# Seven block products for a down projection, with a later start of each group and bias tables made first

## The chip, the cores and the metric

One core of one Trainium2 chip runs the kernel. The metric is the device time of one execution in microseconds, here the median of three runs. TensorE is called PE (its weight loads PEld), VectorE DVE, ScalarE ACT, GpSimd POOL and SyncE SP, as in the profile.

## The reference, cut to what matters

The network has two layers; each is a feed-forward block, a mixer (attention, dilated attention, gated delta rule) and a second feed-forward block. The change concerns the four feed-forward blocks and the small bias tables of the dilated attention.

```python
def swiglu(x, wg, wu, wd):
    return (jax.nn.silu(x @ wg) * (x @ wu)) @ wd

for l in range(DEPTH):   # DEPTH = 2, x: 512 x 1024, wg and wu: 1024 x 2816, wd: 2816 x 1024, float32
    h = h + 0.5 * swiglu(rms_norm(h, ffn1_norm[l]), ffn1_w_gate[l], ffn1_w_up[l], ffn1_w_down[l])
    h = h + hybrid_mixer(rms_norm(h, mix_norm[l]), rel_bias, ...)
    h = h + 0.5 * swiglu(rms_norm(h, ffn2_norm[l]), ffn2_w_gate[l], ffn2_w_up[l], ffn2_w_down[l])
```

## The kernel before

Everything is held transposed: eight tiles x[0..7] of 128 features by 512 tokens, so a matmul has a 128x128 block of weights as its loaded operand and 512 tokens as its moving one. Each float32 product is made of three matmuls (mm3, L214 to L218): weights and activations are split into a high part of type float32r and the rest, and high times high, high times rest and rest times high are summed in PSUM. The split of a weight block (weight, L200) is a DMA on SP, a copy on ACT (L210) and a subtraction on DVE (L211); it is issued at high priority, so it stands early in those queues.

A feed-forward block (ffn, L270) goes over 22 row blocks f of the hidden layer in groups of 8, 7 and 7. For each f it makes the gate and the up product (8 mm3 each, tile pg), then s and h on DVE, ACT and POOL (L294 to L298), and the split of h (hh, hl, L301 and L302). After each group come eight down products, one for each output tile dm: the group's 7 or 8 mm3 into tile pd, and an addition of half of it to x[dm] on DVE (L310). That is 8 x 22 x 3 = 528 down matmuls of 512 columns in a block, 2,112 in the program. In the last group norm_add (L231) follows each dm: it scales, splits and squares x[dm] for the next norm, and norm_end (L247) sums the squares on PE.

The bias tables: build_lines (L176) loads three small tables, makes one row by head with a matmul (pline, L193), writes it to memory and spreads it over 128 rows there (L198). It is called inside the first feed-forward block, before its fourth f (L278).

The program is written through a scheduler that orders each engine's instructions; an engine then works through its own queue in that order and waits at the head of it.

Of the kernel before, what the change touches and what calls it, by code (L numbers as in the profile page):

```python
# [19 lines left out]
P = 128  # L20
# [6 lines left out]
FGROUPS = [8, 7, 7]  # L27
AHEAD = 1
HOLD = 5
SCAN_AT = (0, 2, 4, 6, 8, 10, 12, 14)  # L30
# [82 lines left out]
class Body:  # L113
    def __init__(self, tc, ctx, a):
# [11 lines left out]
        self.ones = self.const.tile([P, P], F32, name="ones")  # L126
# [37 lines left out]
    def load_consts(self):  # L164
# [4 lines left out]
        self.pick = self.const.tile([64, 6 * P], F32R, name="pick")  # L169
        self.ident16 = self.const.tile([P, P], BF16, name="ident16")  # L170
# [5 lines left out]
    def build_lines(self, ps=None):  # L176
        nc = self.nc
        self.line = self.dram.tile([6, P * (2 * T + 1)], F32, name="line")
        one = self.dram.tile([6, NLINE], F32, name="oneline")
        with self.tc.tile_pool(name="lines", bufs=1) as lp, (nullcontext(ps) if ps else self.banks("lp")) as ps:  # L180
            pick = lp.tile([64, 6 * P], F32, name="pick")
            nc.scalar.dma_start(out=pick, in_=self.a["pick"])
            nc.scalar.activation(out=self.pick, in_=pick, func=AF.Copy)
# [6 lines left out]
            for c0 in range(0, NLINE, T):  # L190
                n = min(T, NLINE - c0)
                p = ps.tile([P, T], F32, name="pline", tag="aux", bufs=3)
                nc.tensor.matmul(out=p[0:6, :n], lhsT=rb, rhs=tab[:, c0:c0 + n], start=True, stop=True)  # L193
                nc.vector.tensor_scalar(out=row[:, c0:c0 + n], in0=p[0:6, :n], scalar1=-1.0, scalar2=None, op0=ALU.mult)
            nc.scalar.dma_start(out=one, in_=row)
        for h in range(6):
            dst = self.line[h:h + 1, :].rearrange("o (p n) -> (o p) n", n=2 * T + 1)[:, 0:NLINE]
            nc.scalar.dma_start(out=dst, in_=one[h:h + 1, :].to_broadcast([P, NLINE]))  # L198

    def weight(self, src, n, tiles=None):  # L200
        nc = self.nc
        if tiles is None:
            raw = self.wp.tile([P, n], F32, name="wraw", tag="wraw", bufs=2)
            hi = self.wp.tile([P, n], F32R, name="whi", tag="whi")
            lo = self.wp.tile([P, n], F32R, name="wlo", tag="wlo")
        else:
            raw, hi, lo = tiles
# [6 lines left out]
    def mm3(self, out, w, x, first, last):  # L214
        nc = self.nc
        nc.tensor.matmul(out=out, lhsT=w[0], rhs=x[0], start=first, stop=False)  # L216
        nc.tensor.matmul(out=out, lhsT=w[0], rhs=x[1], start=False, stop=False)  # L217
        nc.tensor.matmul(out=out, lhsT=w[1], rhs=x[0], start=False, stop=last)  # L218
# [12 lines left out]
    def norm_add(self, n, i):  # L231
# [6 lines left out]
        n["x"].append((hi, lo))  # L238
        if i == 0:
# [7 lines left out]
    def norm_end(self, n, ps):  # L247
        nc = self.nc
        pb = ps.tile([P, T], F32, name="pssq", tag="aux", bufs=3)
        for t in range(NT):  # L250
            for r in (0, 64):
                nc.tensor.matmul(out=pb[r:r + 64, t:t + 1], lhsT=n["acc"][:, t * P + r:t * P + r + 64],
                                 rhs=self.ones[:, 0:1], start=True, stop=True)
# [5 lines left out]
        pr = ps.tile([P, T], F32, name="prow", tag="aux", bufs=3)  # L259
# [10 lines left out]
    def ffn(self, n, wgu, wd, nxt):  # L270
        nc, tc = self.nc, self.tc
        scope = lambda name, bufs: tc.tile_pool(name=name, bufs=bufs, reuse_waits="tile")
        with scope("fs", 2) as fs, scope("fh", max(FGROUPS)) as fh, self.banks("fp") as ps:
            f0 = 0
            for gi, ng in enumerate(FGROUPS):
                hs = []
                for f in range(f0, f0 + ng):
                    if self.hold and f == 3:  # L278
                        self.build_lines(ps)
                    pp = []  # L280
                    for which in range(2):
                        hold = self.tc.issue_after(self.hold) if self.hold and f + which == 1 else nullcontext()
                        with hold:
                            hi, lo = self.weight(wgu[f, :, which], D)
                        p = ps.tile([P, T], F32, name="pg", tag="mm")
                        pp.append(p)
                        for k in range(KD):
                            c = slice(k * P, k * P + P)
                            self.mm3(p, (hi[:, c], lo[:, c]), n["x"][k], k == 0, k == KD - 1)
# [769 lines left out]
```

## Time and profile before

| | us |
|---|---|
| runs, median (three, 2237.58 to 2239.57) | 2239.5 |
| the profiled execution, its own time | 2234.65 |
| its span in the profile | 2232.6 |
| PE busy | 2179.1 |
| PE weight loads busy | 1745.9 |
| DVE, ACT, POOL busy | 1138.8, 789.5, 483.7 |

The span is what the trace covers of an execution. An engine is busy while it works on an instruction; matmuls overlap each other, so their length (397 ns for 512 columns) is more than their spacing, and it is the spacing that counts for time.

### The profile page before, as it was taken

How to read it: one execution, taken by the hardware profiler on the slowest of the kernel's cores; microseconds unless marked ns; L12 is line 12 of the kernel's file. 1: busy time of each engine (PE TensorE's matmuls, PEld its weight loads, DVE VectorE, ACT ScalarE, POOL GpSimd, SP SyncE). 2: the span in 40 equal slices, each digit the busy share in tenths (PEclk: the TensorE clock that was granted, in tenths of full speed). 3: DMA queues.
4: the chain of work that ended last, by engine and by line, in shares of the span. 5: the costliest groups of instructions: out<-in, count | busy, mean ns of one | idle time of the engine just before them, and what ended most of it. 6: DMA issues, size and time to landing. Idle time of an engine off the chain costs nothing.

```text
span 2232.6 us, 30294 instructions
## 1 busy us (share of the span) xinstructions
PE 2179.1 (98%) x12212; PEld 1745.9 (78%) x12212; DVE 1138.8 (51%) x1881; ACT 789.5 (35%) x1153; POOL 483.7 (22%) x490
## 2 busy tenths in 40 slices
PE   7999999998999999999999999999989999999999
PEld 5888887778777888888788888877787778888887
DVE  5333334688677533333443333347795765333333
ACT  4222223524565322222332222235345643222221
POOL 3101012217253210101121010123073531101010
PEclk9999999999999999999999999999999999999999
DMA  5433333232302333333233333332331033333333
GB/s 172 127 95 94 96 95 120 81 82 85 92 18 95 95 94 95 95 90 98 86 95 94 95 91 98 92 126 67 100 103 47 28 105 92 94 93 93 96 92 102
DMA packets 93076, 206.82 MB, mean 93 GB/s; under 512 B 38561, under 2 KB 39073, under 8 KB 92936
## 3 DMA queue, kind: packets, MB, share of 16 engines
q1 hardware_dynamic: 91168, 199.98, 30.0%
q10 hardware_dynamic: 1768, 4.91, 0.8%
q8 instruction: 96, 1.57, 0.3%
q14 instruction: 44, 0.36, 0.1%
HBM read 193.83 MB, written 14.18 MB: 93 GB/s over the span
## 4 chain that ended last, share of the span: by engine, by line
PE 88%; DVE 8%; ACT 2%; issue 1%; DMA 1%; POOL 0%; ACTq 0%; SPq 0%; DVEq 0%; POOLq 0%
PE pg L218 15%; PE pg L216 15%; PE pg L217 15%; PE pd L218 7%; PE pd L216 7%; PE pd L217 7%; PE pc L216 2%; PE pc L218 2%; PE pc L217 2%; PE pav L900 1%; PE ppt L894 1%; DVE wlo L211 1%; PE pwo L217 1%; PE pwo L216 1%; PE pwo L218 1%
## 5 line engine op out<-in xcount | busy, mean ns | idle before, releaser
L210 ACT ACTIVATE whi<-wraw 128x1024 fp32r<-128x1024 f32 (+3 forms) x344 | 351.4, 1022 | 1228.9 <-PE pg L217 651.7
L216 PE MATMUL pg<-xh,whi 128*128 128x512 f32 x1408 | 558.0, 397 | 8.5 <-ACT xh L236 8.3
L217 PE MATMUL pg<-xl,whi 128*128 128x512 f32 x1408 | 558.4, 397 | 2.3 <-DVE xl L237 2.2
L218 PE MATMUL pg<-xh,wlo 128*128 128x512 f32 x1408 | 557.8, 396 | 0.8 <-DVE wlo L211 0.8
L211 DVE TENSOR_TENSOR wlo<-wraw,whi 128x1024 fp32r<-128x1024 f32 (+3 forms) x344 | 408.4, 1187 | 89.0 <-ACT whi L210 83.5
L296 POOL TENSOR_TENSOR s<-s,rstd 128x512 f32<-128x512 f32 x88 | 152.7, 1737 | 1146.5 <-ACT s L295 1146.5
L216 PEld LDWEIGHTS pg<-xh,whi 128*128 128x128 f32 x1408 | 265.2, 188 | 73.2 <-ACT xh L236 8.3
L217 PEld LDWEIGHTS pg<-xl,whi 128*128 128x128 f32 x1408 | 265.0, 188 | 68.5 <-DVE xl L237 5.3
L218 PEld LDWEIGHTS pg<-xh,wlo 128*128 128x128 f32 x1408 | 265.1, 188 | 65.1 <-DVE wlo L211 1.9
L218 PE MATMUL pd<-hh,wlo 128*128 128x512 f32 x704 | 278.7, 396 | 0.9 <-DVE wlo L211 0.9
L216 PE MATMUL pd<-hh,whi 128*128 128x512 f32 x704 | 278.5, 396 | 0.0
L217 PE MATMUL pd<-hl,whi 128*128 128x512 f32 x704 | 278.4, 395 | 0.0
L310 DVE SCALAR_TENSOR_TENSOR x<-pd,x 128x512 f32<-128x512 f32 x96 | 66.3, 691 | 284.6 <-PE pd L218 284.6
L298 DVE TENSOR_TENSOR h<-pg,s 128x512 f32<-128x512 f32 x88 | 60.9, 691 | 287.8 <-PE pg L218 281.3
L294 DVE TENSOR_TENSOR s<-pg,rstd 128x512 f32<-128x512 f32 x88 | 60.6, 691 | 229.9 <-PE pg L218 229.7
L218 PEld LDWEIGHTS pd<-hh,wlo 128*128 128x128 f32 x704 | 132.3, 188 | 34.0 <-DVE wlo L211 2.2
L217 PEld LDWEIGHTS pd<-hl,whi 128*128 128x128 f32 x704 | 132.4, 188 | 31.9
L216 PEld LDWEIGHTS pd<-hh,whi 128*128 128x128 f32 x704 | 132.4, 188 | 31.7
L753 PE MATMUL pgr<-wlo,xh 128*128 128x384 f32 (+1 forms) x256 | 92.0, 360 | 11.2 <-DVE wlo L211 11.1
L884 POOL TENSOR_TENSOR prob<-prob,sm 128x512 f32<-128x512 f32 x80 | 84.6, 1066 | 78.5 <-DVE sm L883 63.5
L245 POOL TENSOR_TENSOR acc<-acc,sq 128x512 f32<-128x512 f32 x42 | 67.5, 1606 | 132.6 <-ACT sq L244 132.0
L754 PE MATMUL pgr<-whi,xl 128*128 128x384 f32 (+1 forms) x256 | 90.7, 354 | 0.0
(235 smaller groups left out, 2702.0 us busy)
## 6 DMA issues: line engine op xcount, KB each, us to landing
wraw<-in_gu_dram SPq DMA_DIRECT2D x176, 512.0 KB, 3.6
wraw<-in_wd_dram SPq DMA_DIRECT2D x64, 448.0 KB, 3.3
wraw<-in_wd_dram SPq DMA_DIRECT2D x32, 512.0 KB, 3.6
wraw<-in_w_c_dram SPq DMA_DIRECT2D x24, 512.0 KB, 3.6
wraw<-in_w_gb_dram SPq DMA_DIRECT2D x24, 384.0 KB, 3.1
wraw<-in_w_o_dram SPq DMA_DIRECT2D x14, 512.0 KB, 3.7
bias<-line SPq DMA_DIRECT2D x12, 448.0 KB, 5.0
saved<-x SPq DMA_DIRECT2D x16, 256.0 KB, 2.0
```

The lines of the kernel that those rows point to most:

```text
L210: nc.scalar.activation(out=hi, in_=raw, func=AF.Copy)
L211: nc.vector.tensor_tensor(out=lo, in0=raw, in1=hi, op=ALU.subtract)
L216: nc.tensor.matmul(out=out, lhsT=w[0], rhs=x[0], start=first, stop=False)
L217: nc.tensor.matmul(out=out, lhsT=w[0], rhs=x[1], start=False, stop=False)
L218: nc.tensor.matmul(out=out, lhsT=w[1], rhs=x[0], start=False, stop=last)
L245: nc.gpsimd.tensor_tensor(out=n["acc"], in0=n["acc"], in1=sq, op=ALU.add)
L296: nc.gpsimd.tensor_tensor(out=s, in0=s, in1=n["rstd"], op=ALU.mult)
L298: nc.vector.tensor_tensor(out=h, in0=pp[1], in1=s, op=ALU.mult)
L310: nc.vector.scalar_tensor_tensor(out=self.x[dm], in0=p, scalar=0.5, in1=self.x[dm], op0=ALU.mult, op1=ALU.add)
L753: nc.tensor.matmul(out=o, lhsT=xh[:, tk], rhs=lo[:, wc], start=False, stop=False)
L754: nc.tensor.matmul(out=o, lhsT=xl[:, tk], rhs=hi[:, wc], start=False, stop=kk == KD - 1)
L884: nc.gpsimd.tensor_tensor(out=pb, in0=pb, in1=sm.to_broadcast([P, T]), op=ALU.mult)
```

## The change

The down projection works on pairs of row blocks and pairs of output tiles. Hidden row blocks f = j and f = j + 11 (HALF) form pair j; output tiles dm and dm + 4 form a pair; the 512 tokens are cut into two halves of 256. Each such 2x2 by 2x2 block product takes seven products instead of eight, on sums and differences of the blocks:

- up makes, for pair j, both gate and up products (unchanged matmuls), then three subtractions on DVE for the combined tokens, and seven split blocks of 256 columns (hh and hl, in a call with four and one with three of them).
- down loads the four weight blocks of a group for the pair dm in two DMAs (ra, rb), makes s1, s2, s4 on POOL and one difference on DVE, splits 7 blocks of weights (ra, sa, rb, s4), and runs seven products of 256 columns on three PSUM tiles, pu, py and pz. pu is added to x by DVE after each of its four products, while PE keeps summing into it. There are 4 steps dm a group, and a group has 3, 4 and 4 pairs.
- a group's down steps come after the up product of one pair more than the group holds (hs[0:ng] is used, one pair stays over). In the last group there is no such pair, and the first step (late) leaves the last pair's matmuls of its first three products to the end of them.
- build_lines is called before the first feed-forward block, right after the constants; the tables' six spread writes stay inside the block, as spread_lines. The next norm takes its tiles in the order 0, 4, 1, 5, 2, 6, 3, 7. In the program there are 4 x 4 x 11 x 7 x 3 = 3,696 down matmuls of 256 columns.

```diff
-FGROUPS = [8, 7, 7]
+FPAIRS = [3, 4, 4]
+HALF = FF // P // 2
+TH = T // 2
+RAWS, SPLITS, MM = 2, 2, 6
...
+            hs, j0 = [], 0
+            for gi, ng in enumerate(FPAIRS):
+                last = gi == len(FPAIRS) - 1
+                for j in range(j0 + len(hs), min(j0 + ng + 1, HALF)):
+                    hs.append(self.up(n, wgu, j, fs, fh, ps))
+                for dm in range(KD // 2):
+                    self.down(wd[dm, :, j0 * 4 * P:(j0 + ng) * 4 * P], dm, hs[0:ng], fs, ps, last and dm == 0)
+                    if last and nxt is not None:
                         self.norm_add(nxt, dm)
-                f0 += ng
+                        self.norm_add(nxt, dm + KD // 2)
+                j0, hs = j0 + ng, hs[ng:]
...
+        t = fs.tile([P, 3, TH], F32, name="ht", bufs=1)
+        sub = lambda out, x, y: nc.vector.tensor_tensor(out=out, in0=x, in1=y, op=ALU.subtract)
+        sub(t[:, 0:2], h[:, 1::2], h[:, 0:2])
+        sub(h[:, 1], h[:, 3], t[:, 0])
+        sub(t[:, 2], h[:, 2], h[:, 1])
+        hh = fh.tile([P, 7, TH], F32R, name="hh")
+        hl = fh.tile([P, 7, TH], F32R, name="hl")
+        for o, src in ((slice(0, 4), h), (slice(4, 7), t)):
+            nc.scalar.activation(out=hh[:, o], in_=src, func=AF.Copy)
+            nc.vector.tensor_tensor(out=hl[:, o], in0=src, in1=hh[:, o], op=ALU.subtract)
+        return hh, hl
+
+    def down(self, src, dm, hs, fs, ps, late):
...
+            ra, rb = self.raw(2 * m), fs.tile([P, 2 * m], F32, name="wrb")
+            nc.sync.dma_start(out=ra, in_=src[:, 0:2 * m])
+            nc.sync.dma_start(out=rb, in_=src[:, 2 * m:4 * m])
+            a11, a12, a22, a21 = ra[:, 0:m], ra[:, m:], rb[:, 0:m], rb[:, m:]
+            sa = fs.tile([P, 2 * m], F32, name="wsa")
+            s4 = fs.tile([P, m], F32, name="wsb", bufs=1)
+            s1, s2 = sa[:, 0:m], sa[:, m:]
+            nc.gpsimd.tensor_tensor(out=s1, in0=a21, in1=a22, op=ALU.add)
+            nc.gpsimd.tensor_tensor(out=s2, in0=s1, in1=a11, op=ALU.subtract)
+            nc.gpsimd.tensor_tensor(out=s4, in0=a12, in1=s2, op=ALU.subtract)
+            nc.vector.tensor_tensor(out=a21, in0=a11, in1=a21, op=ALU.subtract)
+            wa, wb = self.halves(ra), self.halves(sa)
+            wc, wd = (self.halves(v, tuple(fs.tile([P, v.shape[-1]], F32R, name=nm + x, bufs=1) for x in "hl"))
+                      for v, nm in ((rb, "wc"), (s4, "wd")))
...
+        begin = (u, wa, 0, 0), (z, wb, 0, 4), (y, wa, 1, 2)
+        if late:
+            for js in (range(ng - 1), range(ng - 1, ng)):
+                for args in begin:
+                    product(*args, True, js)
+        else:
+            product(*begin[0], True)
+            product(*begin[1], True)
+        h5 = fs.tile([P, TH], F32, name="p5", bufs=1)
+        add(0, u)
+        nc.scalar.activation(out=h5, in_=z, func=AF.Copy, scale=0.5)
+        product(u, wb, 1, 1, False)
+        add(1, u)
+        if not late:
+            product(*begin[2], True)
+        add(0, y)
+        product(u, wc, 1, 5, False)
+        add(3, u)
+        nc.gpsimd.tensor_tensor(out=x[3], in0=x[3], in1=h5, op=ALU.add)
+        product(z, wd, 0, 3, False)
+        add(1, z)
+        product(u, wc, 0, 6, False)
+        add(2, u)
...
             k.load_consts()
+            k.build_lines()
```

The scheduler decides where these stand in the queues; three places matter below. The first is ACT's queue in the program's first microseconds (xh and sq belong to the first norm, whi is the high part of a gate or up weight block). Before:

```order
L161 DMA small_71<-in_small_dram 128x96
L182 DMA pick<-in_pick_dram 64x768
L186 DMA rb<-in_rel_bias_dram 32x6
L210 ACT_TABLE_LOAD
L210 ACTIVATE whi<-wraw 128x1024
L188 DMA tab<-in_line_table_dram 33x1023
L236 ACTIVATE xh<-x,small_71 128x512
```

and with the change, from the last xh on:

```order
L256 ACTIVATE xh<-x,small_71 128x512
L164 DMA small_147<-in_small_dram 128x96
L170 DMA consts<-in_consts_dram 128x1794
L265 ACTIVATE sq<-x 128x512
L175 DMA pick<-in_pick_dram 64x768
L265 ACTIVATE sq<-x 128x512
L176 ACTIVATE pick<-pick 64x768
L190 DMA rb<-in_rel_bias_dram 32x6
L192 DMA tab<-in_line_table_dram 33x1023
L199 DMA oneline<-row 6x1023
L205 DMA line<-oneline 128x1023 x6
L216 ACTIVATE whi<-wraw 128x1024 x2
```

The loads of rb and tab have moved from the front of the queue to behind the copy of pick. PE's queue now begins with the matmuls that need them:

```order
L197 MATMUL pline<-tab,rb 6x512
L197 MATMUL pline<-tab,rb 6x511
L236 MATMUL pg<-xh,whi 128x512
L237 MATMUL pg<-xl,whi 128x512
L238 MATMUL pg<-xh,wlo 128x512
```

Before, pline stood behind 98 other rows of this queue; now the first pg matmul stands behind pline.

The second place is DVE's queue where the last group of a feed-forward block begins (s and h belong to the last pair; wlo is the rest part of wa, then of wb):

```order
L329 TENSOR_TENSOR s<-pg,rstd 128x512
L231 TENSOR_TENSOR wlo<-wraw,whi 128x1024
L333 TENSOR_TENSOR h<-pg,s 128x512
L335 TENSOR_TENSOR ht<-h 128x512
L231 TENSOR_TENSOR wlo<-wsa,whi 128x1024
L335 TENSOR_TENSOR h<-h,ht 128x256
L335 TENSOR_TENSOR ht<-h 128x256
L361 TENSOR_TENSOR wrb<-wraw,wrb 128x512
L343 TENSOR_TENSOR hl<-h,hh 128x1024
L343 TENSOR_TENSOR hl<-ht,hh 128x768
L376 SCALAR_TENSOR_TENSOR x<-pu,x 128x256
```

and before, at the same place:

```order
L294 TENSOR_TENSOR s<-pg,rstd 128x512
L211 TENSOR_TENSOR wlo<-wraw,whi 128x896
L298 TENSOR_TENSOR h<-pg,s 128x512
L211 TENSOR_TENSOR wlo<-wraw,whi 128x896
L302 TENSOR_TENSOR hl<-h,hh 128x512
L310 SCALAR_TENSOR_TENSOR x<-pd,x 128x512
```

Between h and the first addition to x there were two instructions; now there are seven, one of which (wrb) waits for POOL.

The third place is PE's queue inside a down step, at the change from one product to the next (with buffer numbers, since pu is used four times):

```order
L238 MATMUL pu_1823<-hh_1646,wlo_1808 128x256
L236 MATMUL pz_1825<-hh_807,whi_1811 128x256
L237 MATMUL pz_1825<-hl_808,whi_1811 128x256
L236 MATMUL py_1824<-hh_807,whi_1807 128x256
L237 MATMUL py_1824<-hl_808,whi_1807 128x256
L238 MATMUL py_1824<-hh_807,wlo_1808 128x256
```

where before stood

```order
L216 MATMUL pd_839<-hh_265,whi_834 128x512
L217 MATMUL pd_839<-hl_266,whi_834 128x512
L216 MATMUL pd_807<-hh_797,whi_802 128x512
L218 MATMUL pd_839<-hh_265,wlo_835 128x512
L216 MATMUL pd_839<-hh_337,whi_834 128x512
```

Each matmul has half as many columns and, as before, a weight load of its own; products of different steps are interleaved.

## Rows read from the trace of the kernel before

**Rows 1.** page, head, busy time and chain of waits by engine

```profile
span 2232.6 us, 30294 instructions
PE 2179.1 (98%) x12212; PEld 1745.9 (78%) x12212; DVE 1138.8 (51%) x1881; ACT 789.5 (35%) x1153; POOL 483.7 (22%) x490
...
PE 88%; DVE 8%; ACT 2%; issue 1%; DMA 1%; POOL 0%; ACTq 0%; SPq 0%; DVEq 0%; POOLq 0%
```

**Rows 2.** windows: us, PE, PEld, DVE, ACT, POOL busy (count), clock, DMA share, GB/s

```profile
232.00:271.00 39.00, 39.00 (x169) 31.43 (x168) 15.00 (x17) 8.39 (x9) 0.00 (x0) 1.00 0.32 93
```

**Rows 3.** PE timeline (start us, us), first and last of 168 down matmuls of a group

```profile
232.16 0.40 PE L216 MATMUL pd<-hh,whi 128*128 128x512 f32 x1
...
271.13 0.39 PE L218 MATMUL pd<-hh,wlo 128*128 128x512 f32 x1
```

**Rows 4.** PE timeline: 384 columns, first and last of seven; then the 128-column ones

```profile
514.98 0.33 PE L753 MATMUL pgr<-wlo,xh 128*128 128x384 f32 x1
...
516.02 0.34 PE L753 MATMUL pgr<-wlo,xh 128*128 128x384 f32 x1
...
36.54 1.06 PE L261 MATMUL prow<-consts,rcol 128*128 128x128 f32 x8
...
L261 PE MATMUL prow<-consts,rcol x8: 273/275/275, 36.5 to 37.3; 128*128 128x128 f32 x8
```

**Rows 5.** weight loads by form: busy us, mean ns

```profile
L216 PEld LDWEIGHTS pd<-hh,whi 128*128 128x128 f32 x704 | 132.4, 188 | 31.7
L261 PEld LDWEIGHTS prow<-consts,rcol 128*128 128x128 f32 x48 | 6.3, 190 | 0.5
```

**Rows 6.** DVE by form: busy us, mean ns | idle before

```profile
L211 DVE TENSOR_TENSOR wlo<-wraw,whi 128x1024 fp32r<-128x1024 f32 x254 | 311.9, 1228 | 69.7 <-ACT whi L210 69.0
L211 DVE TENSOR_TENSOR wlo<-wraw,whi 128x768 fp32r<-128x768 f32 x24 | 23.3, 972 | 13.6 <-ACT whi L210 13.6
L302 DVE TENSOR_TENSOR hl<-h,hh 128x512 fp32r<-128x512 f32 x88 | 60.2, 686 | 0.8 <-ACT hh L301 0.7
L537 DVE TENSOR_TENSOR kd<-pt,ek 128x384 f32<-128x384 f32 x16 | 7.9, 547 | 1.0 <-PE pt L534 1.0
L776 DVE TENSOR_TENSOR qkv<-qkv,rqg 128x256 f32<-128x256 f32 x24 | 8.6, 416 | 0.1
```

**Rows 7.** ACT by form: busy us, mean ns | idle before

```profile
L210 ACT ACTIVATE whi<-wraw 128x1024 fp32r<-128x1024 f32 x254 | 269.3, 1061 | 966.8 <-PE pg L217 587.8 <-PE pd L217 174.0 <-issue 75.5
L210 ACT ACTIVATE whi<-wraw 128x768 fp32r<-128x768 f32 x24 | 20.2, 843 | 27.2 <-PE pgr L754 17.1 <-DMA wraw<-in_w_gb_dram 6.5 <-DVE wlo L211 3.3
```

**Rows 8.** POOL: one line, ns min/median/max; then the 384-column form, mean ns

```profile
L296 POOL TENSOR_TENSOR s<-s,rstd x88: 1277/1790/2452, 39.8 to 2185.7; 128x512 f32<-128x512 f32 x88
...
L562 POOL TENSOR_TENSOR gt<-g,consts 128x384 f32<-128x384 f32 x16 | 17.0, 1067 | 7.5 <-DVE g L469 4.7 <-PE pe L566 2.8
```

**Rows 9.** windows of the gate and up matmuls alone, from the start

```profile
0.00:30.00 30.00, 17.98 (x58) 11.62 (x59) 0.00 (x0) 1.00 0.62 189
```

**Rows 10.** timeline of the start, all engines

```profile
8.29 0.79 PE L216 MATMUL pg<-xh,whi 128*128 128x512 f32 x1 [8.29 <-ACT xh L236]
17.67 0.44 ACTq L167 DMA_DIRECT2D consts<-in_consts_dram  x1
...
23.34 0.21 DVE L171 CAST ident<-consts 128x128 bf16<-128x128 f32 x1
...
39.86 1.88 PE L193 MATMUL pline<-tab,rb 33*6 33x512 f32 x4
...
43.96 0.30 ACTq L195 DMA_DIRECT2D oneline<-row  x1
...
46.57 1.19 ACTq L198 DMA_DIRECT2D line<-oneline  x2
```

**Rows 11.** DMA issues: count, KB each, median us to landing

```profile
consts<-in_consts_dram ACTq DMA_DIRECT2D x1, 897.0 KB, 4.7
pick<-in_pick_dram ACTq DMA_DIRECT2D x1, 192.0 KB, 7.4
```

More of the change, by code (lines that the diff above doesn't have):

```diff
@@ L169, in load_consts @@
         self.pick = self.const.tile([64, 6 * P], F32R, name="pick")
+        with self.tc.tile_pool(name="picks", bufs=1, reuse_waits="tile") as lp:
+            pick = lp.tile([64, 6 * P], F32, name="pick")
+            nc.scalar.dma_start(out=pick, in_=self.a["pick"])
+            nc.scalar.activation(out=self.pick, in_=pick, func=AF.Copy)
         self.ident16 = self.const.tile([P, P], BF16, name="ident16")
@@ L174, in load_consts, with build_lines @@
         nc.vector.tensor_copy(out=self.mask16[:, 1], in_=self.c["mask_r"])
-    def build_lines(self, ps=None):
+    def build_lines(self):
         nc = self.nc
         self.line = self.dram.tile([6, P * (2 * T + 1)], F32, name="line")
[L179 to L183, printed above, removed]
+        self.one = one = self.dram.tile([6, NLINE], F32, name="oneline")
+        with self.tc.tile_pool(name="lines", bufs=1, reuse_waits="tile") as lp, self.banks("lp") as ps:
             rb = lp.tile([33, 6], F32, name="rb")
@@ L202, in weight @@
         if tiles is None:
-            raw = self.wp.tile([P, n], F32, name="wraw", tag="wraw", bufs=2)
-            hi = self.wp.tile([P, n], F32R, name="whi", tag="whi")
-            lo = self.wp.tile([P, n], F32R, name="wlo", tag="wlo")
+            raw = self.raw(n)
+            hi, lo = self.split(n)
         else:
@@ new lines, in up @@
+    def up(self, n, wgu, j, fs, fh, ps):
+        nc = self.nc
+        h = fs.tile([P, 4, TH], F32, name="h")
+        for half in range(2):
+            f = j + half * HALF
+            if self.hold and (j, half) == (2, 0):
+                self.spread_lines()
+            pp = []
+            for which in range(2):
+                first = j == half == 0
+                hold = self.tc.issue_after(self.hold) if self.hold and first and which else nullcontext()
+                with hold:
+                    hi, lo = self.weight(wgu[f, :, which], D)
+                p = ps.tile([P, T], F32, name="pg", tag="mm", bufs=MM)
+                pp.append(p)
+                for i, k in enumerate(n["order"]):
+                    c = slice(k * P, k * P + P)
+                    self.mm3(p, (hi[:, c], lo[:, c]), n["x"][k], i == 0, i == KD - 1)
+                if which == 0:
+                    if first:
+                        self.norm_end(n, ps, 2)
+                    s = fs.tile([P, T], F32, name="s")
+                    nc.vector.tensor_tensor(out=s, in0=p, in1=n["rstd"], op=ALU.mult)
+                    nc.scalar.activation(out=s, in_=s, func=AF.Silu)
+                    nc.gpsimd.tensor_tensor(out=s, in0=s, in1=n["rstd"], op=ALU.mult)
+            hv = h[:, 2 * half:2 * half + 2].rearrange("p a t -> p (a t)")
+            nc.vector.tensor_tensor(out=hv, in0=pp[1], in1=s, op=ALU.mult)
+        t = fs.tile([P, 3, TH], F32, name="ht", bufs=1)
[9 more added lines that the diff above has]
+        return hh, hl
```

106 lines of the change are left out of this document (50 added, 56 removed).

## The prediction, made before the changed kernel had run

> **What bounds the kernel now.** The page comes first: PE is busy 98% of the span and the chain of waits runs through PE for 88% of it, so what the kernel loses or gains is PE time [rows 1]. The windows of single stages say the same of the stage that changes: in 39 us of the second down group of the first block PE is busy for all 39, DVE for 15.0, ACT for 8.4 and POOL not at all [rows 2]. DVE and POOL have room there, PE has none. What one matmul costs is read not from its length (0.40 us) but from starts in the timeline: 168 down matmuls begin between 232.16 and 271.13, which is 38.97 / 167 = 0.2333 us each [rows 3]. So all 2,112 down matmuls cost 492.7 us, and nothing else in their stage is on the path.
>
> **What the products cost.** The change puts 3,696 matmuls of 256 columns in place of 2,112 of 512. No 256-column float32r matmul is in the trace, so its price lies between neighbours. Six steps of 384 columns take 516.02 - 514.98 = 1.04 us, 0.1733 each [rows 4]. From 512 to 384 columns the spacing falls by 0.0600; a second fall of the same size gives 0.1133 for 256. Whether the weight load, one for every matmul, lets it fall so far is seen at the eight 128-column matmuls of prow: first start to last end 1.06 us, less the last one's 0.274, over seven, is 0.112 each, although each of them brings a 128x128 load of 190 ns mean, as long as the 188 of the down projection's [rows 4, 5]. So loads can follow each other every 0.112 us. I take 0.1133: 418.8 us, a gain of **73.9**. The ends are 0.112 (gain 78.7) and half of the 512-column price, 0.1167 (gain 61.4).
>
> A rule of the Trainium skill speaks against this. Its page "TensorE: Matmul & The Clock Gate", section "The mechanism" of Part 3, says that weight loads overlap running matmuls only when they go to another row group, which these full-height loads never do. By it a load of about 107 ns (its section "LDWEIGHTS (loading the stationary operand)": columns / 1.2, an estimate here) would be added to every matmul. Then 0.126 of the 0.2333 would be streaming, 256 columns would take 0.107 + 0.063 = 0.170 and the products 629 us, 136 more than now. The trace does not agree: 384 columns would take 0.202, and take 0.1733.
>
> **The start of the program.** PE's first instruction is now pline, which needs rb and tab; their loads stand on ACT behind the copy of pick, whose load stands behind that of consts. Before, consts is issued at 17.67 and takes 0.44 to issue [rows 10], so pick is issued at about 18.1. It lands after 4.7 us (what consts itself took) at 22.8, or after 7.4 (what pick took beside other loads) at 25.5 [rows 11]. I take 22.8, since what competes is mainly consts, done by 23.34 [rows 10]. The copy has 768 columns, 0.84 us [rows 7]: 23.7. Two issues and a small load are about 3.2 us (oneline, issued at 43.96, lets the next one go at 46.57, 2.6 us; a line issue is 0.6) [rows 10]: pline starts near 27. It took 1.88 us in full swing [rows 10], and about twice that on an engine that has just begun, where the first matmul took 0.79 instead of 0.40 [rows 10, 3]. So gate and up matmuls begin near **30** instead of at 8.29. Before, 58 of them had begun by 30 us [rows 9]: 58 x 0.2333 = 13.5 us behind. Pline's 1.9 later on is saved, and some slow matmuls cost 1.4: **+13**, ends +10 and +17. ACT then issues the spread of the lines, up to about 38 us, before its next whi; PE's first 48 matmuls last until about 42, so that wait is covered.
>
> **The start of the last group.** There no spare pair stands between the last pair's matmuls and its use. From their end, DVE's order is h (0.69), ht (0.69), wlo (1.23), h (0.42): 3.03 us [rows 6]. ACT then copies 1024 and 768 columns, 1.06 and 0.84, to 4.9 [rows 7]. DVE meanwhile does ht (0.42) and wrb (0.69), which waits for POOL's s1; that can begin at 2.6, when wlo frees the buffer, and takes 1.28 at least [rows 8]. Then the two hl, 1.23 and 0.97 [rows 6], end at about 7.0. PE can fill 27 matmuls of the first three products and 7 more, 3.85 us. It waits 3.2, with four hand-overs of about 0.1 some **3.5 us** in each of four blocks: **+14**; ends +6 (no wait for POOL, ACT ahead) and +20.
>
> **Hand-overs inside the steps.** A step of four pairs has 84 matmuls, 9.52 us; DVE has three splits of 1024 columns (3.68), two operations on 512 (1.37) and six additions of 256 (2.50), together 7.55 [rows 6]. A step of three pairs: 63 matmuls, 7.14 us; DVE 2.92 + 1.09 + 2.50 = 6.51 [rows 6]. DVE goes from 38% of the stage to 79% and 91%. Each product into pu waits for the addition before it, with one product (1.36 or 1.02 us) between. I walked through the queues of the first and the second group with these durations: in the first, DVE is late with a wlo by 0.1 and 1.25 us; in the second by 0.1 to 0.5. With POOL in DVE's way at times I take 1.5 us a group, for 12 groups: **+18**. The lower end is 4; the upper end belongs to the second rival. The last step of each block ends with two products into the same pu with nothing between, so PE waits for one addition, 0.42 + about 0.2: **+2**.
>
> **Costed at nothing.** POOL's three operations a step (1.3 to 1.8 us each on 512 columns [rows 8]) are done a step ahead; their cover is the earlier step, and without it each would stand before a wlo. The DMAs carry the same bytes, two pieces for a step that is about twice as long as an output tile was. The subtractions in up and the splits of 1792 columns have a whole pair's matmuls (22.4 us) in the first two groups. The last norm has two tiles to take at the end instead of one, but only x[7] is late, behind 21 matmuls of the next stage.
>
> **Sum.** -73.9 + 13 + 14 + 18 + 2 = -27 us. The profiled execution's own time is 2234.65, so 2208; the median of the runs shown is 2239.5, 4.9 above it, and from that I predict **2213**. What a measurement of this kernel can tell from no change is about 0.2%, 4.5 us.
>
> **Rivals.** *First: hand-overs hidden.* DVE stays ahead and the last group's wait is 2 us: -78 + 10 + 8 + 4 + 1 = -55, 2185. For it: DVE has idle gaps even in the three-pair step. Against it: 91% is little room for a queue that works in strict order.
>
> *Second: DVE and POOL become the bound of the down steps, and the kernel is slower.* POOL's s product on the same sizes takes between 1277 and 2452 ns, median 1790 [rows 8]; the most is the least plus one DVE split of 1.23 [rows 6], as if one held up the other. If every POOL operation (three of about 1.28 and 0.7 for an addition to x, 4.5 us a step; for three pairs three of 1.07 and 0.64, 3.8) keeps DVE out, a step needs 12.05 against 9.52 and 10.3 against 7.14: 2.5 x 32 + 3.2 x 16 = 132 us instead of 18 + 14. That is -73.9 + 13 + 132 + 2 = +73, 2313. It decides from a loss of about 59 us in the steps, under half of it. Against it: part of each group's POOL work is done before the group. For it: three-pair steps stand at the limit already. The Trainium skill's page "SBUF — State Buffer", section "Who interferes with whom", has the rule behind it: a DVE operation with two SBUF inputs and a POOL operation that reads SBUF hold a shared port in turn, and the second waits for the whole first. The spread of the s product agrees.
>
> *Third: the weight load sets the spacing, and the kernel is slower.* With 0.188 us, a load's whole length [rows 5], the products cost 695: +202 and the waits' 47, 2488. It decides from 0.121 (2,112 x 0.2333 less 47, over 3,696), only 0.008 above my price. Prow at 0.112 speaks against it, but those are eight matmuls at a time and read fewer columns. The skill's rule above has a milder form of it, 2239.5 + 136 + 47 = 2422.
>
> **How the numbers follow.** Forecast case (steps and starts losing 20 to 65 us in all, price near 0.1133): 0.48. First rival: 0.14. Second, half of it or more: 0.16; its milder part is still near no change. Third, any price over 0.121: 0.10. The rest, 0.12, is a longer start or a scheduler's order that costs elsewhere, of either sign. Faster by over 0.2%: 0.48 + 0.14 + 0.08 = 0.70; within 0.2%: 0.09; slower: 0.21. The range starts at the first rival's 2185 and reaches to 2258, where the ends of the unknown costs meet: -70 for the products, +17, +20, +2 and 50 for the steps. What is left out is most of the second rival and the third.
>
> **What would show it.** In the profile after: 256-column rows pu, py and pz whose starts lie 0.113 apart (0.12 or more: third rival); PE idle until about 27 us, with the first idle ended by the tables' DMA; three or four us before each last group's hl; idle before products on pu ended by DVE's additions or wlo, about 20 us in all; POOL near 6 us a step. If DVE is busy over 95% of the down stages and PE waits there for more than 60 us, the second rival holds. If pg starts near 10 us, my start is wrong.

## The result, and the profile after

The changed kernel takes 2276.8 us (median of four runs, 2272.1 to 2306.4; without the highest, a disturbed run that the ratio leaves out, the median is 2273.2) against 2239.5 for the kernel before beside it: ratio **1.0159**, 95% interval 1.0132 to 1.0186. It is slower, where 2213 and faster was forecast. The profiled execution took 2273.2, 38.6 more than the one before.

The page's head, busy time and chain of the changed kernel, beside [rows 1]:

```profile
span 2271.4 us, 34477 instructions
PE 2154.6 (95%) x13796; PEld 1804.5 (79%) x13796; DVE 1454.6 (64%) x2349; ACT 915.1 (40%) x1301; POOL 740.1 (33%) x682
...
PE 73%; DVE 14%; issue 5%; DMA 3%; ACT 3%; POOL 3%; SPq 0%; DVEq 0%; ACTq 0%; POOLq 0%
```

PE is busy 24.5 us less than before in a span 38.8 us longer, and of the 15% of the chain of waits that has left PE, 6 have gone to DVE and 4 to issue. What PE now waits for (line, then releaser: us in total, times, longest):

```profile
PE pline L197 <- DMA tab<-in_line_table_dram: 26.1, 1, 26.1
PE pz L238 <- DVE wlo L231: 17.2, 8, 2.6
...
PE pu L236 <- DVE x L376: 11.9, 11, 2.0
PE pu L238 <- DVE wlo L231: 5.8, 7, 1.1
PE pu L237 <- DVE hl L343: 5.4, 4, 1.4
```

The start is the first row. In the timeline of the changed kernel (start us, us), against [rows 10]:

```profile
20.97 0.62 ACTq L192 DMA_DIRECT2D tab<-in_line_table_dram  x1
26.09 3.57 PE L197 MATMUL pline<-tab,rb 33*6 33x512 f32 x4 [26.09 <-DMA tab<-in_line_table_dram]
...
29.59 0.79 PE L236 MATMUL pg<-xh,whi 128*128 128x512 f32 x1
```

Gate and up matmuls begin at 29.59 instead of 8.29, and the two hundredth of them at 79.8 instead of 65.8. The rest of the loss lies in the three down groups. Their stretches in the first block (us, PE, PEld, DVE, ACT, POOL busy with counts, clock, DMA share, GB/s):

```profile
123.00:165.90 42.90, 41.68 (x298) 38.65 (x297) 32.08 (x48) 16.75 (x23) 17.05 (x13) 1.00 0.34 105
245.00:297.70 52.70, 49.70 (x378) 47.48 (x377) 35.22 (x49) 19.02 (x23) 21.20 (x15) 1.00 0.33 101
355.50:409.20 53.70, 45.45 (x337) 43.50 (x337) 43.33 (x54) 25.78 (x36) 27.20 (x24) 0.91 0.30 96
```

In the first two stretches gate and up matmuls of the next pair are mixed in. Below, the time of a group is its stretch from first to last down matmul, less 0.2333 us for each gate or up matmul between: 32.3, 43.2 and 53.5 us here. A group of three pairs has 252 down matmuls and one of four 336, so the two equal groups differ by 10 us. All twelve groups take 514.8 us, against 491.7 before. The sum is 13.4 for the start (from the experiment on it, below) and 23.1 for the groups, 36.5 of the 38.6 us.

### The profile page after: what moved, and what is told of

The parts are those of the page before. It is cut to its first block, busy times and chain, and to the rows that moved or that the text cites. A ratio compares the mean times of both kernels' runs of the same rounds, so it can differ in the third digit from the quotient of the medians.

```text
span 2271.4 us, 34477 instructions
## 1 busy us (share of the span) xinstructions
PE 2154.6 (95%) x13796; PEld 1804.5 (79%) x13796; DVE 1454.6 (64%) x2349; ACT 915.1 (40%) x1301; POOL 740.1 (33%) x682
## 4 chain that ended last, share of the span: by engine, by line
PE 73%; DVE 14%; issue 5%; DMA 3%; ACT 3%; POOL 3%; SPq 0%; DVEq 0%; ACTq 0%; POOLq 0%
PE pg L236 13%; PE pg L237 13%; PE pg L238 12%; PE pu L238 3%; PE pu L236 3%; PE pu L237 3%; PE pc L236 2%; PE pc L238 2%; PE pc L237 2%; DVE wlo L217 1%; PE pav L986 1%; DVE wlo L231 1%; PE ppt L980 1%; PE pz L238 1%; PE pz L236 1%
## 5 line engine op out<-in xcount | busy, mean ns | idle before, releaser
L216 ACT ACTIVATE whi<-wraw 128x1024 fp32r<-128x1024 f32 (+2 forms) x248 | 256.2, 1033 | 726.3 <-PE pg L237 436.4
L217 DVE TENSOR_TENSOR wlo<-wraw,whi 128x1024 fp32r<-128x1024 f32 (+2 forms) x248 | 312.9, 1262 | 83.9 <-ACT whi L216 80.7
L376 DVE SCALAR_TENSOR_TENSOR x<-pu,x 128x256 f32<-128x256 f32 x192 | 79.2, 417 | 99.5 <-PE pu L238 99.0
L236 PE MATMUL pu<-hh,wch 128*128 128x256 f32 x352 | 102.2, 290 | 9.7 <-DVE x L376 9.7
L238 PE MATMUL pu<-hh,wlo 128*128 128x256 f32 x352 | 103.6, 295 | 6.3 <-DVE wlo L231 5.8
L237 PE MATMUL pu<-hl,whi 128*128 128x256 f32 x352 | 102.7, 292 | 5.4 <-DVE hl L343 5.4
L360 POOL TENSOR_TENSOR wsb<-wraw,wsa 128x512 f32<-128x512 f32 (+1 forms) x48 | 85.6, 1784 | 63.9 <-DVE wdl L231 61.3
L236 PE MATMUL pu<-hh,whi 128*128 128x256 f32 x352 | 102.5, 292 | 3.5 <-DVE x L376 2.2
L238 PE MATMUL pu<-hh,wcl 128*128 128x256 f32 x352 | 101.1, 287 | 1.2 <-DVE wcl L231 1.0
L237 PE MATMUL pu<-hl,wch 128*128 128x256 f32 x352 | 100.9, 287 | 0.0
```

What stands on the lines that cost most here:

```text
L216: nc.scalar.activation(out=hi, in_=raw, func=AF.Copy)
L217: nc.vector.tensor_tensor(out=lo, in0=raw, in1=hi, op=ALU.subtract)
L360: nc.gpsimd.tensor_tensor(out=s4, in0=a12, in1=s2, op=ALU.subtract)
L376: nc.vector.scalar_tensor_tensor(out=x[i], in0=p, scalar=0.5, in1=x[i], op0=ALU.mult, op1=ALU.add)
```

## The experiments

| kernel | us, median | ratio to before, 95% | twelve groups, us |
|---|---|---|---|
| the change, tables made at once | 2261.7 | 1.0085 to 1.0134 | 515.6 |
| the kernel before, tables as in the change | 2251.8 | 1.0047 to 1.0089 | 491.7 |
| the change without POOL's sums | 2225.2 | 0.9920 to 0.9963 | 467.1 |
| the change, POOL's sums unused | 2281.1 | 1.0168 to 1.0218 | 519.7 |
| the change without the spare pair | 2315.6 | 1.0321 to 1.0364 | 555.6 |
| tables at once, last pair first | 2266.7 | 1.0108 to 1.0155 | 514.7 |
| tables at once, last group plain | 2225.5 | 0.9925 to 0.9961 | 474.4 |
| the same, groups 4-4-3 | 2228.1 | 0.9951 to 0.9976 | 477.0 |
| the same, sums on DVE | **2202.3** | 0.9825 to 0.9864 | 456.1 |
| the change, sums on DVE | 2245.2 | 1.0021 to 1.0048 | 484.0 |

**The start.** Two kernels: the change with the tables made before x is loaded, and the kernel before with the change's place for the tables.

```diff
 sm = [k.load_small(0)]
+k.build_lines()
 ...
-            k.build_lines()
```

> The changed kernel, but the bias tables' loads (rb, tab) are issued at the head of ACT's queue instead of behind the copy of pick. Theory (the start costs what it delays): the first gate matmul moves from 29.6 us back to about 10 us and the time falls by 12 to 15 us, to about 2260. Rival (the late start is regained later, because weights or norms would have held PE up anyway): the first gate matmul is early, but the time falls by less than 4 us.

> The kernel before with this one part of the change: pick, rb and tab loaded behind the constants, and the line matmuls at the head of PE's queue. Theory: it costs 12 to 15 us by itself, 2252 to 2255. Rival (cost belongs to the new down projection's loads at the start): under 4 us.

The second shows the start by itself: its groups take the 491.7 us of the kernel before, its first gate matmul begins at 28.2 and its median is 13.4 us above that of the kernel before beside it. In the first kernel the tables' loads stand ahead of everything on ACT's queue:

```profile
1.66 0.63 ACTq L192 DMA_DIRECT2D tab<-in_line_table_dram  x1
7.46 3.57 PE L197 MATMUL pline<-tab,rb 33*6 33x512 f32 x4 [7.46 <-DMA tab<-in_line_table_dram]
13.50 0.76 PE L236 MATMUL pg<-xh,whi 128*128 128x512 f32 x1 [2.47 <-DVE row L198]
```

PE begins 18.6 us earlier (the first gate matmul at 13.5, where about 10 was expected), the two hundredth gate or up matmul 11.6, and the profiled run is 12.5 us shorter, while the groups stay at 515.6. The start is settled, and is apart from the rest.

**The price of a matmul.** A kernel of nothing but mm3, 192 matmuls of each width, 512 and 256 columns taken twice, each with its own weight load; everything else of the network is left out.

> Only matmuls: 192 each of 512, 512, 384, 320, 256, 192, 128 and 256 columns, float32r, every one with a 128x128 weight load, nothing else on the chip's engines; the rest of the computation is left out. Theory (the 0.1175 us of the down products belongs to the matmul and its load): 256 columns go at 0.115 to 0.120 us here too. Rival (it comes from what runs beside it): 0.112 to 0.1135 here. Both: 512 at 0.233, 384 at 0.173. If loads set a floor, 192 and 128 columns stay near 0.11; if not, they fall to 0.09 and below.

Its PE timeline at the first and last of 177 matmuls of 512 columns at full clock, then at the first and last matmuls of three widths:

```profile
60.29 0.39 PE L236 MATMUL n512b<-xh,whi 128*128 128x512 f32 x1
...
100.58 0.39 PE L238 MATMUL n512b<-xh,wlo 128*128 128x512 f32 x1
...
100.80 0.34 PE L236 MATMUL n384c<-xh,whi 128*128 128x384 f32 x1
...
133.91 0.34 PE L238 MATMUL n384c<-xh,wlo 128*128 128x384 f32 x1
...
162.24 0.28 PE L236 MATMUL n256e<-xh,whi 128*128 128x256 f32 x1
...
184.74 0.28 PE L238 MATMUL n256e<-xh,wlo 128*128 128x256 f32 x1
...
206.27 0.24 PE L236 MATMUL n128g<-xh,whi 128*128 128x128 f32 x1
...
227.57 0.28 PE L238 MATMUL n128g<-xh,wlo 128*128 128x128 f32 x1
```

Over 191 steps that is 0.1734 us for 384 columns, 0.1178 for 256 and 0.1115 for 128 (192 columns: 0.1116). The 512-column matmuls come every 0.229 (40.29 us over 176 steps), where 0.233 was expected. From 512 to 384 and from 384 to 256 columns the fall is the same, 0.0556; below that the spacing stops at 0.1115. So 256 columns cost 0.118 with nothing beside them, as they do in the changed kernel, and the 3,696 products take 436.1 us. What the groups take beyond that, 78.7 us, is waiting, and in the last groups also matmuls at a slower clock (below).

**POOL's sums.** First they were left out: the second and fourth split take blocks of weights that came by DMA, so three of the four left sides are other blocks than the sums, while ACT, DVE and PE do as much as before.

```diff
-            nc.gpsimd.tensor_tensor(out=s1, in0=a21, in1=a22, op=ALU.add)
-            nc.gpsimd.tensor_tensor(out=s2, in0=s1, in1=a11, op=ALU.subtract)
-            nc.gpsimd.tensor_tensor(out=s4, in0=a12, in1=s2, op=ALU.subtract)
+            s4 = a12
-            wa, wb = self.halves(ra), self.halves(sa)
+            wa, wb = self.halves(ra), self.halves(rb)
```

> The changed kernel without POOL's three sums in each down step: the second and fourth pair of weight blocks are split as they were loaded, so the output is not the reference's; DVE, ACT and PE do the same number of operations. Theory A (POOL stands in DVE's way and its sums come late): DVE's stretched instructions go back to their shortest, the last group falls from 53.5 to about 45 us, and the time falls by 30 us or more, under 2243. Theory B (DVE's own queue, its order and the missing spare pair in the last group, sets the waits): the last group stays over 49 us and the time falls by less than 15 us.

Theory A. The groups fall by 47.7 us; the first and middle ones to 30.0 and 39.7, which is 252 and 336 times 0.118 to within 0.3: hardly a wait is left there. The last ones stay at 46.6 to 48.0, where about 45 was expected. Then POOL made as many sums of the same size that nobody reads:

```diff
-            nc.gpsimd.tensor_tensor(out=s1, in0=a21, in1=a22, op=ALU.add)
+            nc.gpsimd.tensor_tensor(out=s1, in0=a11, in1=a12, op=ALU.add)
-            wa, wb = self.halves(ra), self.halves(sa)
+            wa, wb = self.halves(ra), self.halves(rb)
-                      for v, nm in ((rb, "wc"), (s4, "wd")))
+                      for v, nm in ((rb, "wc"), (a12, "wd")))
```

> The changed kernel (profiled 2273.2 us; all down stages together 514.8 us), but what POOL adds is read by nobody: POOL makes three sums of the same size and number from the first half of the same weights into the same tiles, and the second and fourth split take weights that came by DMA instead of the sums. So three of the four left sides are wrong sums and the output is not the reference's; the work of DVE, ACT, POOL and PE is as long as in the changed kernel. It tells apart why POOL's sums cost about 48 us (the kernel without them took 2225.2 us, its down stages 467.1 us). Theory A, POOL's sums are late and PE waits for the splits that read them: the time falls to near 2225 us (2220 to 2235), down stages near 467 us, although POOL is as busy as before. Theory B, POOL's sums slow DVE's instructions while they run: the time stays near 2273 us (2263 to 2280), down stages near 515 us, and DVE's 1024-column subtractions still show lengths well over 1228 ns. A value between tells the shares.

Theory B: all of the time is back, 2281. DVE's instructions by form (busy us, mean ns, idle before), of the changed kernel, beside [rows 6]:

```profile
L231 DVE TENSOR_TENSOR wlo<-wraw,whi 128x1024 fp32r<-128x1024 f32 x32 | 46.0, 1437 | 2.6 <-ACT whi L230 2.6
...
L361 DVE TENSOR_TENSOR wrb<-wraw,wrb 128x512 f32<-128x512 f32 x32 | 38.7, 1208 | 20.2 <-DMA wraw<-in_wd_dram 16.4 <-POOL wsa L358 3.9
```

without POOL's sums:

```profile
L231 DVE TENSOR_TENSOR wlo<-wraw,whi 128x1024 fp32r<-128x1024 f32 x32 | 39.0, 1218 | 2.9 <-ACT whi L230 2.5
...
L356 DVE TENSOR_TENSOR wrb<-wraw,wrb 128x512 f32<-128x512 f32 x32 | 24.7, 770 | 27.5 <-DMA wraw<-in_wd_dram 16.0 <-DMA wrb<-in_wd_dram 11.2
```

and with sums that nobody reads:

```profile
L231 DVE TENSOR_TENSOR wlo<-wrb,whi 128x1024 fp32r<-128x1024 f32 x32 | 48.6, 1520 | 4.4 <-ACT whi L230 4.4
L231 DVE TENSOR_TENSOR wlo<-wraw,whi 128x1024 fp32r<-128x1024 f32 x32 | 46.9, 1465 | 6.9 <-ACT whi L230 6.8
```

The same subtraction takes 1218 ns with POOL out of the way and 1437 to 1520 beside it, read or unread. So it is not that the sums come late to their readers; it is that POOL has this work to do at that time. Late weight loads are not it either: DVE waits for them before wrb for 34.3 us in the changed kernel, 29.5 with unread sums and 52.5 without sums. Two effects that the traces show are left, and this run has both: DVE's instructions get longer beside POOL's, and s, which POOL makes as well, comes behind the sums in its queue (DVE waits before h for POOL's s 24.7 us in all in the changed kernel, 31.2 with unread sums, 5.3 without sums).

**The last group.** The middle and the last group have the same down matmuls; the last has no spare pair and, in three of the four blocks, carries the next norm. One kernel takes the spare pair from all groups:

```diff
-                for j in range(j0 + len(hs), min(j0 + ng + 1, HALF)):
+                for j in range(j0 + len(hs), min(j0 + ng, HALF)):
-                    self.down(..., last and dm == 0)
+                    self.down(..., dm == 0)
```

> The changed kernel (2273.2 us; groups of 32.4, 43.4 and 53.5 us), with no group begun one pair later: each group's products begin as soon as its own last pair of gate/up tiles is made, in the order that the change uses only for the last group. Theory A, the last group is 10 us longer than the middle one because no spare pair of gate/up products covers the wait for its last pair's splits: now the first and the middle group get the same wait, 5 to 9 us each, in all 8 groups, and the time is 2273 + 40 to 70 = 2313 to 2343 us, with a granted clock of 0.5 after each of these waits. Theory B, the last group is longer because of the next norm's work on DVE, ACT and POOL: the first and middle groups stay within 2 us of 32.4 and 43.4 us, and the time is 2265 to 2289 us.

Theory A, at its lower end: first groups of 35.7 to 36.9 us (32.3 before), middle ones of 48.4 to 48.9 (43.3), so 3.5 to 5.7 us more each where 5 to 9 were expected, and the clock now falls near the start of all twelve groups. Windows of the first two groups and of one such fall:

```profile
100.20:152.40 52.20, 49.05 (x318) 45.01 (x318) 32.06 (x50) 17.68 (x24) 13.73 (x13) 0.93 0.31 95
226.80:286.80 60.00, 54.92 (x385) 51.22 (x384) 35.48 (x49) 20.38 (x24) 21.55 (x15) 0.94 0.29 88
...
104.90:111.70 6.80, 6.09 (x26) 5.80 (x27) 5.46 (x9) 2.86 (x5) 0.00 (x0) 0.50 0.15 32
```

What the wait consists of stands in DVE's timeline of the changed kernel where the first block's last group begins (the last gate or up matmul starts at 355.32; the releaser of an idle time in brackets):

```profile
357.96 0.69 DVE L333 TENSOR_TENSOR h<-pg,s 128x512 f32<-128x512 f32 x1 [2.43 <-POOL s L331]
358.69 0.69 DVE L335 TENSOR_TENSOR ht<-h 128x512 f32<-128x512 f32 x1
359.30 1.22 DVE L231 TENSOR_TENSOR wlo<-wsa,whi 128x1024 fp32r<-128x1024 f32 x1
360.43 0.42 DVE L335 TENSOR_TENSOR h<-h,ht 128x256 f32<-128x256 f32 x1
360.88 1.39 DVE L335 TENSOR_TENSOR ht<-h 128x256 f32<-128x256 f32 x1
362.20 1.75 DVE L361 TENSOR_TENSOR wrb<-wraw,wrb 128x512 f32<-128x512 f32 x1
363.88 1.21 DVE L343 TENSOR_TENSOR hl<-h,hh 128x1024 fp32r<-128x1024 f32 x1
365.01 0.94 DVE L343 TENSOR_TENSOR hl<-ht,hh 128x768 fp32r<-128x768 f32 x1
```

and in POOL's:

```profile
354.53 2.16 POOL L360 TENSOR_TENSOR wsb<-wraw,wsa 128x512 f32<-128x512 f32 x1
356.65 1.28 POOL L331 TENSOR_TENSOR s<-s,rstd 128x512 f32<-128x512 f32 x1
360.59 1.40 POOL L358 TENSOR_TENSOR wsa<-wrb 128x512 f32<-128x512 f32 x1 [2.66 <-DVE wlo L231]
362.07 1.33 POOL L359 TENSOR_TENSOR wsa<-wsa,wraw 128x512 f32<-128x512 f32 x1
```

POOL's third sum (wsb) stands ahead of s, so h starts 2.1 us later than without the sums (there 0.50 us after that last matmul's start, here 2.64). Then ht takes 1.39 instead of 0.42 while the first sum runs, and wrb 1.75 instead of 0.69 over the second: 2.0 us more. PE's own waits, from its starts, are 2.5 for wlo, 1.5 for hh and 1.8 for hl, 5.8 in all, and some 15 matmuls after them come 0.21 apart instead of 0.118, which is 1.5 more. The next kernel makes hl before wlo (on top of tables at once):

```diff
-            wa, wb = self.halves(ra), self.halves(sa)
+            wa = self.halves(ra)
+            with self.tc.issue_after(self.hl.ins) if late else nullcontext():
+                wb = self.halves(sa)
...
-                for args in begin:
+                for args in begin[0::2]:
                     product(*args, True, js)
+            product(*begin[1], True)
```

> The changed kernel with the tables made at once (2261.7 us; last groups of 53.7 us), and in the first step of each last group DVE makes the last pair's halves before it splits the sums, with the order of the products fitted to that (the first two products' last pair together, the third product whole after them). Theory A, the last group's long wait is for DVE, which does the weights' split and the sums' split between the last pair's halves, and the granted clock falls after that wait: with the halves made first the wait shrinks by about 2 us and the drop of the clock behind it (6.8 us at half speed, so 3.4 us) may go too: last groups of 48 to 51 us, time 2241 to 2252 us. Theory B, the wait only moves to the next operand and the clock falls as before: last groups of 53 us or more, time 2257 us or more.

Theory B. PE's waits at the same place are now:

```profile
348.51 0.38 PE L236 MATMUL pu<-hh,whi 128*128 128x256 f32 x1 [2.88 <-ACT hh L342]
349.77 0.39 PE L237 MATMUL pu<-hl,whi 128*128 128x256 f32 x1 [0.76 <-DVE hl L343]
351.76 0.58 PE L236 MATMUL pu<-hh,whi 128*128 128x256 f32 x1 [0.98 <-ACT whi L230]
```

The wait has changed its operand, the clock still falls for 6.8 us behind it, and the last groups take 49.8 to 54.5 us instead of 50.3 to 54.9. Putting the chain in another order did not shorten it.

**What follows from it: less of the change.** The last group goes back to 512-column products on the same weight layout; seven products are made only where a spare pair covers the start. For the last group's pairs up leaves out the three subtractions and splits four blocks instead of seven.

```diff
+                if last:
+                    for dm in range(KD):
+                        ...
+                        hi, lo = self.weight(wd[dm % (KD // 2), :, c0:c0 + 2 * m], 2 * m)
+                        p = ps.tile([P, T], F32, name="pd", tag="mm", bufs=MM)
+                        for j in range(2 * ng):
+                            ...
+                            self.mm3(p, (hi[:, c], lo[:, c]), x, j == 0, j == 2 * ng - 1)
```

> The changed kernel with the tables made at once (2261.7 us; 515.6 us in the down stages), with the last group of every block done by the plain product of 512 columns, as the kernel before does it, and seven products only in the first two groups, where the spare pair covers the start. The last group is then 8 steps x 24 matmuls x 0.2333 us = 44.8 us in place of 53.7 (50.3 in the last block), no sums on POOL in it. Theory A, the last group's loss is its start without cover, POOL's sums and the clock that falls after the waits: all of it goes, the down stages take 4 x (32.4 + 43.3 + 44.8) = 482 us and the time is 2261.7 - 33.6 = 2228 us (2222 to 2235), faster than before by 0.3 to 0.7%. Theory B, the loss lies in the norm's work, which stays: last groups of 50 us or more, time 2250 us or more.

Theory A, and faster than the kernel before. The last group of the first block, norm included:

```profile
340.00:385.00 45.00, 45.00 (x194) 36.22 (x194) 20.37 (x24) 15.99 (x22) 11.31 (x11) 1.00 0.41 133
```

PE has no gap and the clock stays at 1.00; all last groups take 44.6 us. Then one pair more for the seven products, and after that the sums on DVE:

```diff
-FPAIRS = [3, 4, 4]
+FPAIRS = [4, 4, 3]
```

> The kernel with the last group done plainly (2225.5 us; groups of 32.3, 41.6 and 44.6 us), with groups of 4, 4 and 3 pairs in place of 3, 4 and 4: one more pair of tiles goes through the seven products. Theory A, each of the two seven-product groups takes what the middle one takes now, 41.6 us, and the plain group 8 x 18 x 0.2333 = 33.6 us: 4 x 116.8 = 467 us in place of 474.4, time 2218 us (2213 to 2223). Theory B, POOL's sums stretch the first group of four pairs to the 43.3 us that the middle one had in the changed kernel, or the three-pair plain steps of 4.2 us are too short for the next norm's work: time 2224 us or more.

```diff
-            nc.gpsimd.tensor_tensor(out=s1, in0=a21, in1=a22, op=ALU.add)
+            nc.vector.tensor_tensor(out=s1, in0=a21, in1=a22, op=ALU.add)
```

(and s2 and s4 likewise)

> As the kernel with groups of 4, 4 and 3 and the last one plain (expected 2218 us), with the three sums of each step made by DVE instead of POOL. DVE gets 3 x 686 = 2.06 us more to do in each of 32 steps: by lengths without a neighbour, 3 x 1228 + 2 x 686 + 6 x 417 + 3 x 686 = 9.6 us of a step whose products take 84 x 0.118 = 9.9 us. Theory A, what costs is that POOL runs beside DVE: DVE's splits go back to 1228 ns, the two groups take 40 to 42 us each, time 2212 to 2222 us. Theory B, what costs is DVE's own load: with 2.06 us more DVE is the bound and each group takes 43 to 46 us, time 2228 to 2250 us.

With POOL the four-pair first groups take 43.2 to 43.5 us and eat the gain (theory B). With DVE both groups go to 40.3 and 39.7, and the time to 2202.3, the best of all kernels here and 10 us below what theory A had at its lower end. The split by form, and the windows of the two groups:

```profile
L231 DVE TENSOR_TENSOR wlo<-wsa,whi 128x1024 fp32r<-128x1024 f32 x32 | 39.0, 1219 | 2.9 <-ACT whi L230 2.9
```

```profile
133.60:187.40 53.80, 53.63 (x394) 50.73 (x393) 40.22 (x58) 19.92 (x24) 5.35 (x5) 1.00 0.32 99
263.70:315.70 52.00, 52.00 (x390) 49.67 (x389) 34.86 (x53) 19.34 (x24) 4.98 (x5) 1.00 0.25 82
```

PE is busy for all of the second and all but 0.17 us of the first. At last the same edit in the change as it was given:

> The changed kernel (2273.2 us; groups of 32.4, 43.4 and 53.5 us) with nothing altered but the engine of the three sums: DVE makes them, 2.06 us more to do per step of four pairs. Theory A, POOL beside DVE is what cost about 48 us in the down stages: by lengths without a neighbour DVE has 8.1 us to do in a step of three pairs (3 x 951 + 2 x 550 + 6 x 417 + 3 x 550) whose products take 63 x 0.118 = 7.4 us, and 9.6 in one of four, whose products take 9.9; so the first group stays at 31 to 33 us, now bound by DVE, the middle one goes to 39.7 to 40.5, the last one, with no spare pair and the norm's work on DVE, to 47 to 52: down stages 473 to 500 us, time 2231 to 2258 us, near 2245. Theory B, DVE's load itself is what cost: 32 steps of 2.06 us and 16 of 1.65 more make 2273 us and over.

2245.2, as theory A worked it out: 31.4 and 40.3 us for the first two groups, 45.0 to 51.8 for the last (47 to 52 expected; the 45.0 is the last block's). The middle group of the first block:

```profile
244.98:298.70 53.72, 53.56 (x395) 50.73 (x394) 39.92 (x58) 19.84 (x24) 5.32 (x5) 1.00 0.32 100
```

DVE is busy for 39.92 us of 53.72, against 35.22 of 52.70 in the change. Over the whole program it is busy 31.5 us more (1486.1 against 1454.6), although it was given sums of 32 x 2.06 + 16 x 1.65 = 92 us: the rest of its work got shorter. An edit of three lines takes 30.8 us off the groups, and the ratio to the kernel before goes from 1.0159 to 1.0034.

## Why the prediction was wrong

- **The start: right.** Gate and up matmuls near 30 and +13 were forecast; 29.59 and 13.4 were measured.
- **The price of 256 columns: mis-sized.** I took 0.1133; it is 0.118, 17.3 us over 3,696 products (gain 55.6, not 73.9). The failed step is "a second fall of the same size": the fall was read between 0.2333, a mean of a stage [rows 3], and 0.1733, six tight steps [rows 4]. Tight 512-column matmuls come every 0.229; the fall is 0.0556, and by the same rule that gives 0.118. The measured price lay just above my upper end, 0.1167.
- **The start of the last group: mis-sized, by steps left out.** "From their end, DVE's order is h" let h begin at once. It waits for s, which stands on POOL behind a step's third sum (wsb, 2.1 us). The two subtractions beside POOL's next sums take 2.0 us more than [rows 6] gave them. So hl ends 10.2 us after the last matmul's end instead of my 7.0; without the sums it is 6.2. PE waits 5.8 us, not 3.5. With the sums on DVE, two of them inside this chain, hl ends 7.1 us after. What no term held is the clock: during that wait it falls to half (0.50, which is 1.2 GHz) for 6.8 us.
- **The block's end: mis-sized.** "One addition, 0.42 + about 0.2", +2 in all: in the three blocks with a next norm the addition before the last product into pu stands on DVE behind the split of one of the next stage's weight blocks and the norm's xl, and PE waits 2.2 us each time, with POOL's sums and without them. That points to the queue's order; no run changed it. The clock falls there too (0.50 from 406.2). DVE's queue at that place:

```profile
403.28 1.22 DVE L217 TENSOR_TENSOR wlo<-wraw,whi 128x1024 fp32r<-128x1024 f32 x1
404.41 1.75 DVE L257 SCALAR_TENSOR_TENSOR xl<-x,small,xh 128x512 fp32r<-128x512 f32 x1
406.09 0.41 DVE L376 SCALAR_TENSOR_TENSOR x<-pu,x 128x256 f32<-128x256 f32 x1
```

- **Hand-overs in the steps: mis-sized.** 1.5 us a group were forecast; the first groups wait 2.5 to 2.8 and the middle ones 3.6 to 3.9 (times less 29.7 and 39.6 us of products). Without POOL's sums they wait 0 to 0.3. Under "Costed at nothing", the step that failed is POOL's three operations: with sums that nobody reads the kernel is as slow (2281.1), and without them 47.7 us of the groups go. What was missing is what they do to DVE and to s.
- **The other two rivals.** The first, hidden hand-overs, is what the first and middle groups do once POOL is out of the way; the last groups still lose 6.9 to 8.4 us. The third decides from 0.121; the lowest spacing is 0.1115 and the price 0.118, so it did not hold, if by little.
- **Together.** Waits and slow matmuls of 78.7 us against 34 (14 + 18 + 2) and products 17.3 dearer: 62 us, which takes 2213 to 2275.
- **The second rival had the mechanism, but not the way it costs time.** It said that POOL keeps DVE out, and that about 59 us of loss decide; 78.7 were lost, 47.7 with the sums, and without the sums the kernel is faster than before (2225.2). But its test, DVE busy over 95% of the down stages, is not met: DVE is busy for 32.08 of 42.9, 35.22 of 52.7 and 43.33 of 53.7 us. DVE did not become the bound by load. Single instructions became longer, and in the chain read above they stood ahead of something PE needed. The Trainium skill's page "SBUF — State Buffer", section "Who interferes with whom", says that the port pair which DVE and POOL share is an exclusive lock, and that a DVE instruction with two SBUF inputs contends with a POOL instruction that reads SBUF. The rows agree: ht starts at 360.88 inside POOL's 1.40 us sum and ends 0.28 us after it, and wrb starts at 362.20 inside the next sum and ends 0.55 us after it; in both, what is left after the sum is 0.14 us under the instruction's own length.

Of the 78.7 us, 47.7 go with POOL's sums and 31 stay, nearly all in the last groups: 7.0, 8.4, 6.9 and 7.4 us without the sums. The first three of these hold the wait at the block's end, 2.2 us. In that trace a granted clock of 0.50 stands near the group's start in the second block for 3.4 us and in the fourth for 6.8, and in the other two not at all. So 4.8 and 4.7 us are left in the blocks without it and 6.2 and 7.4 in those with it. From these an estimate: about 4.7 us a group for the rest, above all the start without a spare pair, and about 0.4 us for each us at the slow clock. (Taking the spare pair from the other groups cost 3.5 to 5.7 us each, with POOL's sums and the slow clock in it.) How the 47.7 divide between longer DVE instructions and s behind POOL's queue is read from single places of the timeline, not shown by a run of its own; no run sets the slow clock apart from the waits.

## What to carry to other kernels

Moving work to an idle engine isn't free when it lengthens the instructions of the engine that feeds TensorE. Here 2.06 us a step more on DVE cost less than the same sums on POOL beside it, so price such work by the lengths of DVE's instructions with that neighbour, not by DVE's free share. Where a faster product shortens its cover, walk the chain into the first product from every engine's queue, including what stands ahead of the first link, and use the faster product only where spare work covers that chain. Take a difference of two prices from measurements of the same kind, both tight.

## What was not expected of the hardware

- With a weight load of 128x128 for each matmul the spacing does not fall below 0.1115 us: it is 0.1116 at 192 columns and 0.1115 at 128, while at 256 (0.118) it still follows the columns. That the load is what sets this floor is likely, but no run with fewer loads shows it.
- A wait of under 3 us at a time in an otherwise full stretch was followed by a granted clock of 0.50 for 6.8 us, at the start of the last group in all four blocks of the changed kernel (in two of the four without POOL's sums) and, where the spare pair was taken away, near the start of all twelve groups (for 3.4 to 10.2 us); the kernel before has no such stretch in its down groups, and neither have the two whose down stages have hardly a gap (last group plain; the same at 4-4-3 with the sums on DVE).
- A subtraction of 1024 columns on DVE takes 1218 to 1228 ns without POOL's sums beside it and 1437 to 1520 on average beside its sums; one of 256 took 1.39 us instead of 0.42.
